# Layer 0's second feed-forward part by seven block products, and its sums of weights copied in batches

## The chip, the cores and the metric

The kernel runs on one core of a Trainium2 chip. The metric is the device time of one execution in microseconds (us); it is taken several times and the median counts. Beside it stands one profiled execution, whose trace gives the start and the duration of each instruction on each engine: PE is TensorE (its matmuls) and PEld its weight loads, DVE is VectorE, ACT ScalarE, POOL GpSimd, and SP the SyncE whose queue issues most DMAs. All products here are fp32 matrices; the reference's tolerance is met by splitting numbers in two, as told below.

## The reference, cut to what matters

Two layers over 512 tokens of width 1024. Layer 0 has a convolution module and then a feed-forward part; layer 1 has windowed attention over a K and V made once, and then a feed-forward part; a norm ends it.

```python
def rmsnorm(x, g):
    xf = x.astype(jnp.float32)
    xf = xf * lax.rsqrt(jnp.mean(xf * xf, axis=-1, keepdims=True) + EPS)
    return (xf * g.astype(jnp.float32)).astype(x.dtype)

def swiglu_ffn(x, w_up, w_down):
    gate, up = jnp.split(x @ w_up, 2, axis=-1)
    return (jax.nn.silu(gate) * up) @ w_down
...
    h = h + swiglu_ffn(rmsnorm(h, norm_ffn[l]), ffn_w_up[l], ffn_w_down[l])
```

`w_up` is 1024 x 5632 (gate and up of 2816 each) and `w_down` 2816 x 1024, one of each for a layer. The change concerns `x @ w_up` of layer 0.

## The kernel before, in words

**Layout and precision.** The residual `h` lies transposed, channels on partitions, 8 tiles of 128 x 512 tokens. Weights lie in DRAM as chunks of 128 x 1024 fp32 (512 KB), in the array `W`. `PLAN` lists the chunks in the order in which PE uses them. For each use `advance` (L274) issues the loads up to nine chunks ahead (`load` L235, on SP, into `raw` buffers, seven of them) and splits chunks up to three ahead (`split_weights` L262): ACT casts `whi` (L263) and DVE subtracts for `wlo` (L266), four buffers of each. `mm3` (L345) then makes one fp32 product of three fp32r matmuls, whi by x-high, whi by x-low, wlo by x-high (L349 to L351). The first chunks (`NATIVE`) are used unsplit, in one fp32 matmul (L347) that reads the raw buffer itself.

**The feed-forward part, a pair at a time.** A pair is 256 of the 2816 hidden columns. Layer 0 takes 11 pairs in two parts (`HALVES0`). Pairs 0 to 4 are done for each half of the tokens as soon as that half's convolution is finished, the first half by `mm3`, the second by `mm2` (L376, two matmuls where one is 512 wide, `twin=True`). Pairs 5 to 10 follow for all 512 tokens at once: `ffn_part(0, 1, x0["ffn0"], ALL, ...)` calls `ffn_up` (L600), which for each pair uses 4 chunks, 8 `mm3` each, 128 x 512 outputs, and then `down_group`.

**Seven products.** Layer 1 (pairs 1 to 10) does the up product by blocks: the weights of a pair are cut in 2 x 2 blocks A11 to A22, the rows of tokens in B11 to B22, and seven products of half the size replace eight (`SEVEN`, L55: A11 B11, S1 T1, S2 T2, A12 B21, S3 T3, S4 B22, A22 T4). T1 to T4 are sums of blocks of x, made once in SBUF by POOL and split by ACT and DVE. S1 to S4 are sums of blocks of weights, made in DRAM by DMA: SP copies one block to a scratch tile (L255) and POOL adds the second by an accumulating DMA (L259). `prepare` (L243) is a generator of those copies and additions; `advance` takes `share[0]` of a step from it for each chunk used. It keeps the addition six steps behind its copy. `seven_pair` (L766) runs the seven products as 168 matmuls of 128 x 256 into three PSUM banks, gathers the four blocks of the result in SBUF (L784 to L796), and applies the norm's scale (L802), silu (L803) and the gate (L804).

**What sets the order.** Instructions are put on the engines' queues by a scheduler that works from the program's order and a modelled time line; each queue then runs in order. `tc.issue_after(x)` keeps an instruction behind another. Side work runs in generators: `job(gen, points)` takes steps from one as chunks are used (`pace` L305), here the convolution of the second half and the reads of the attention bias (`read_bias` L1189). The POOL queue carries arithmetic and the additions' DMAs, so an addition that waits for its copy holds what stands behind it.

**The stages in the trace.** Convolution and its pointwise products up to about 129 us, `pw2` and pairs 0 to 4 of the first half to 265, `pw2` and pairs 0 to 4 of the second half to 362, the up products of pairs 5 to 10 to 493 and their down products to 558, K, V and attention to 718, layer 1's feed-forward part to 1043, the end to 1058. DRAM tables for the bias are written in the convolution stage (`table_in` L1093, `table` L1099: `fd`, 3 MB).

Of the kernel before, what the change touches and what calls it, by code (L numbers as in the profile page):

```python
# [18 lines left out]
P = 128  # L19
# [39 lines left out]
def by_seven(layer, pair):  # L59
    return layer == 1 and pair in SEVENS  # L60
# [56 lines left out]
BLOCKS = [c[:2] + (f"A{a}",) for c in PLAN if len(c) == 3 and c[2] == "S1" for a in (11, 12, 21, 22)]  # L117
# [5 lines left out]
def lay_weights(w):  # L123
    out = np.empty((len(CHUNKS), P, 1024), np.float32)
    q = w["w_q"][0][:, HEAD_COLS]
    o = w["w_o"][0][HEAD_COLS, :]
    for i, c in enumerate(CHUNKS):
        if c[0] == "pw1":
            t = w["conv_w_pw1"][0][:, c[1] * P:(c[1] + 1) * P].reshape(KT, P, P)
        elif is_block(c):  # L130
            m, k = int(c[2][1]) - 1, int(c[2][2]) - 1
            if c[0] == "up":
                t = [w["ffn_w_up"][1][k * 512:(k + 1) * 512, col:col + P].reshape(4, P, P)
                     for col in (e * FF + c[1] * 256 + m * P for e in range(2))]
# [56 lines left out]
def hybrid_trunk(ctx: ExitStack, tc: tile.TileContext, xT, W, prm_in, wdw_in, sinks, relb, onehot, fin, lead, out):  # L191
# [33 lines left out]
    summed, preparing, share, loaded = {}, [iter(())], [0, 0], []  # L225
# [4 lines left out]
    def chunk(c, name=None):  # L230
        if name is not None:
            c = c[:2] + (name,)
        return summed[c] if is_sum(c) else W[CHUNK_AT[c]]

    def load(upto):  # L235
        while stream["dma"] < min(len(PLAN), upto):
            i = stream["dma"]
            r = wpool.tile([P, 1024], F32, tag="raw", name=uid("raw"), bufs=7)
            loaded[:] = [nc.sync.dma_start(r, chunk(PLAN[i])).ins]
            raws[i] = r  # L240
            stream["dma"] += 1

    def prepare():  # L243

        units = [c[:2] for c in PLAN if is_block(c) and c[2] == "S1"]
        adds, todo, before = [], [], None
        for u in units:
            adds += [u + ("S1",), *([before + ("S4",)] if before else []), u + ("S2",), u + ("S3",)]
            before = u
        adds.append(before + ("S4",))  # L250
        for c in adds + [None] * 6:
            if c is not None:
                summed[c] = dpool.tile([P, 1024], F32, tag=uid("sum"), name=uid("sum"))
                with tc.issue_after(loaded[0]):
                    nc.sync.dma_start(summed[c], chunk(c, SUMS[c[2]][0]))  # L255
                todo.append(c)
            if c is None or len(todo) > 6:
                a = todo.pop(0)
                nc.gpsimd.dma_start(summed[a], chunk(a, SUMS[a[2]][1]), accum_op=ALU.add, max_dma_last_dim=4096)  # L259
            yield  # L260
# [132 lines left out]
    both = [wpool.tile([P, 1024], F32, tag="raw", name=uid("both"), bufs=7) for _ in range(KT // 2)]  # L393
# [53 lines left out]
    class Rms:  # L447
# [6 lines left out]
        def add(self, t):  # L454
            sq = temp()[:, 0:self.w]
            self.squared = nc.scalar.square(sq, t).ins
            if self.acc is None:
                self.acc = sq
            else:
                self.eng.tensor_add(sq, self.acc, sq)  # L460
                self.acc = sq

        def step1(self):
# [10 lines left out]
            nc.gpsimd.tensor_tensor(self.rs[:, 0:n], ms[:, 0:n], mhalf[:, 0:n], op=ALU.pow)  # L474
# [77 lines left out]
    def ffn_part(layer, part, xg, tok, rms, on_h=None, twin=False, plain=None):  # L552
# [3 lines left out]
        for g in range(2):  # L556
            if twin:
# [11 lines left out]
                for m, b in enumerate(banks):  # L569
                    t, hm = temp()[:, 0:w], h[g * 4 + m][:, tok]  # L570
                    nc.scalar.copy(t, b[:, 1, :])
                    nc.vector.tensor_add(t, b[:, 0, :], t)
                    nc.gpsimd.tensor_mul(t, t, rs_bc)
                    nc.vector.tensor_add(hm, hm, t)
# [24 lines left out]
    def ffn_up(layer, lo, hi, xg, tok, rms, twin=False, plain=None):  # L599
# [3 lines left out]
        def evac(pair, banks):  # L603
            rs_bc = rms.step2()
            if twin:
# [10 lines left out]
                nc.gpsimd.tensor_mul(t2, t1, t2)  # L616
# [15 lines left out]
            for m in range(2):  # L632
# [4 lines left out]
                nc.gpsimd.tensor_mul(t2, t1, t2)  # L637
# [65 lines left out]
    class Rows:  # L703


        def __init__(self, gain, pool):
# [3 lines left out]
            self.block = {f"B{j + 1}{s + 1}": [q[:, :, HALF[s]] for q in self.x.q[j]] for j in range(2) for s in range(2)}  # L710
# [5 lines left out]
        def sums(self):  # L716
# [7 lines left out]
            for name, t, f, a, b in (("T1", t1, nc.gpsimd.tensor_sub, b11, b12), ("T2", b11, nc.gpsimd.tensor_add, b22, t1),  # L724
                                     ("T3", b12, nc.gpsimd.tensor_sub, b22, b12), ("T4", b21, nc.gpsimd.tensor_sub, b11, b21)):
                f(t, a, b)
                yield
                both = quads.tile([P, 2, 4, 256], F32R, tag="quad", name=uid("rows"))
                self.block[name] = [both[:, a] for a in range(2)]
                split(self.block[name], t, name == "T2")  # L730
# [35 lines left out]
    def seven_pair(pair, rows, pool, between=None):  # L766

        c = new_gates(pool)
        c11, c12, c21, c22 = (c[:, m, s] for m in range(2) for s in range(2))
        chains = {}  # L770
        for n, name in enumerate(SEVEN):
            w = [x.rearrange("p (a k c) -> p a k c", a=2, k=4) for x in get_seven("up", pair, n)]
# [6 lines left out]
            for which in range(2):  # L779
                for k in range(4):  # L780
                    mm3(r[:, which], [v[:, which, k, :] for v in w], [x[e][:, k, :] for e in range(2)],
# [18 lines left out]
        for m in range(2):  # L800
# [3 lines left out]
            nc.gpsimd.tensor_mul(gate, gate, c[:, m, :, 1, :])  # L804
# [4 lines left out]
    def forms_of(c, pool, odd):  # L809
# [7 lines left out]
        for t, a, b in (("T1", "B11", "B12"), ("T3", "B22", "B12"), ("T2", "B22", "T1"), ("T4", "T2", "B21")):  # L817
            (nc.gpsimd.tensor_add if t == "T2" else nc.gpsimd.tensor_sub)(f[:, FORM[t]], f[:, FORM[a]], f[:, FORM[b]])
# [10 lines left out]
    def low_pairs(pair, forms, rs):  # L829

        chains = {}
        for n, name in enumerate(SEVEN):
# [6 lines left out]
            for t, out in enumerate(chains[chain]):  # L839
# [8 lines left out]
                if a == "A12":  # L848
                    m = temp()
                    nc.scalar.mul(m, out, scale)  # L850
                    nc.gpsimd.tensor_add(to, to, m.rearrange("p (i c) -> p i c", i=4))
# [24 lines left out]
    with tc.tile_pool(name="conv", bufs=2) as cv:  # L876
# [41 lines left out]
        class Half:  # L918
# [7 lines left out]
            def taps(self, ct, c):  # L926
# [9 lines left out]
                for i in range(nd):  # L936
                    while pi * nd < n_pool * (i + 1):
# [4 lines left out]
                        else:  # L942
                            on_act = nc.scalar.mul(pr, a[:, j:j + W2], tap(j))  # L943
                            on_pool = nc.gpsimd.tensor_add(pr, acc, pr)  # L944
# [10 lines left out]
                nc.gpsimd.tensor_add(yt, yt, acc)  # L955
# [137 lines left out]
        def table_in():  # L1093
            nc.sync.dma_start(sk, sinks.to_broadcast([P, NH]))
            nc.sync.dma_start(lhs[0:NBUCKET, :], relb)
            nc.sync.dma_start(oh, onehot)
            nc.gpsimd.memset(lhs[NBUCKET:NBUCKET + 1, :], NEG)

        def table():  # L1099
# [4 lines left out]
            nc.sync.dma_start(fd.rearrange("q h k -> h q k"), fs.unsqueeze(1).to_broadcast([NH, P, 3 * P]))  # L1104
# [77 lines left out]
        pw2(h0.z, n0)  # L1182
        ffn_part(0, 0, x0["ffn0"], HALF[0], n0.rms, plain=plain)
        flush()

    attn = ExitStack()
    at = attn.enter_context(tc.tile_pool(name="attn", bufs=2))
# [11 lines left out]
    base = seen[0]  # L1199
# [6 lines left out]
    class Both:  # L1206
        def step1(self):
            pass
# [3 lines left out]

    nxt = Next(("kv", "mix1"))


    share[0] = 1 / 2
    if True:
        ffn_part(0, 1, x0["ffn0"], ALL, Both(), nxt.on_h)
# [60 lines left out]
        def pair(gp, jp, n0):  # L1279
# [33 lines left out]
            for (n, k0, nk), sc, m4 in zip(units, scs, m4s):  # L1313
# [6 lines left out]
                for j in range(4):  # L1320
                    nc.gpsimd.tensor_scalar(sc[:, j, 1:1 + w], sc[:, j, 1:1 + w], sm[:, j:j + 1], 0.0,
                                            op0=ALU.mult, op1=ALU.add)
# [104 lines left out]
    share[0] = 1 / 3  # L1427
    for kind, pair in STEPS1:
# [6 lines left out]
        if by_seven(1, pair):  # L1435
            c = seven_pair(pair, nxt, pool7, flip if pair == SEVENS[0] else None)
# [70 lines left out]
```

## Time and profile before

| | |
|---|---|
| runs | 1059.93, 1061.91, 1062.57 us; median 1061.91 |
| the profiled execution | 1060.15 us, span 1058.4 us from the first to the last instruction |
| granted TensorE clock | 0.996 |
| matmuls in the trace | 6166 |
| DMA | 211.04 MB in packets, mean 199 GB/s |

The profile page gives busy times, the span in 40 slices, the DMA queues, the chain of waits that ended last, and the costliest groups of instructions. A group's line reads: source line, engine, operation, output and inputs, shape, count; then busy time and the mean of one in ns; then the idle time before them and what ended it. A plain fp32 matmul stands in the trace as two records, an fp32r one as one.

### The profile page before, as it was taken

How to read it: one execution, taken by the hardware profiler on the slowest of the kernel's cores; microseconds unless marked ns; L12 is line 12 of the kernel's file. 1: busy time of each engine (PE TensorE's matmuls, PEld its weight loads, DVE VectorE, ACT ScalarE, POOL GpSimd, SP SyncE). 2: the span in 40 equal slices, each digit the busy share in tenths (PEclk: the TensorE clock that was granted, in tenths of full speed). 3: DMA queues.
4: the chain of work that ended last, by engine and by line, in shares of the span. 5: the costliest groups of instructions: out<-in, count | busy, mean ns of one | idle time of the engine just before them, and what ended most of it. 6: DMA issues, size and time to landing. Idle time of an engine off the chain costs nothing.

```text
span 1058.4 us, 16667 instructions
## 1 busy us (share of the span) xinstructions
PE 1046.2 (99%) x6166; PEld 923.3 (87%) x6166; DVE 737.6 (70%) x1163; ACT 576.6 (54%) x1008; POOL 437.8 (41%) x535
## 2 busy tenths in 40 slices
PE   9999999999999999999999999999999999999996
PEld 8888889999988888888888877778989999898995
DVE  3999988977866654454427466678678777868677
ACT  3887897854645423322325465556655555554653
POOL 3999999810333312221124255305242323323131
PEclk9999999999999999999999999999999999999998
DMA  9438045577999996767779876765799565555532
GB/s 354 153 96 98 7 140 199 182 225 218 278 291 293 327 256 183 213 164 192 204 210 247 239 199 172 187 164 170 239 274 305 185 196 174 170 194 183 195 121 80
DMA packets 56606, 211.04 MB, mean 199 GB/s; under 512 B 6891, under 2 KB 13196, under 8 KB 55564
## 3 DMA queue, kind: packets, MB, share of 16 engines
q1 hardware_dynamic: 47164, 177.42, 49.8%
q0 software_dynamic: 8640, 31.46, 16.9%
q8 instruction: 48, 0.79, 0.3%
q10 hardware_dynamic: 720, 1.10, 0.3%
q14 instruction: 34, 0.28, 0.1%
HBM read 204.71 MB, written 68.16 MB: 258 GB/s over the span
## 4 chain that ended last, share of the span: by engine, by line
PE 89%; ACT 4%; issue 2%; POOL 2%; DVE 1%; DMA 1%; SPq 0%; ACTq 0%; POOLq 0%
PE bank L349 19%; PE bank L351 19%; PE bank L350 19%; PE bank L844 9%; PE bank L902 8%; PE bank L381 5%; PE bank L382 3%; ACT pr L943 1%; PE bank L1302 1%; PE bank L1344 1%; PE bank L1331 1%; PE bank L1000 1%; DMA sum<-in_W_dram 1%; POOL pr L944 1%; DMA both<-in_lead_dram 1%
## 5 line engine op out<-in xcount | busy, mean ns | idle before, releaser
L266 DVE TENSOR_TENSOR wlo<-raw,whi 128x1024 fp32r<-128x1024 f32 x231 | 305.8, 1332 | 166.1 <-ACT whi L263 165.1
L263 ACT CAST whi<-raw 128x1024 fp32r<-128x1024 f32 x231 | 241.2, 1049 | 274.8 <-PE bank L350 194.4
L349 PE MATMUL bank<-quad,whi 128*128 128x256 f32 (+1 forms) x976 | 326.9, 336 | 0.0
L350 PE MATMUL bank<-quad,whi 128*128 128x256 f32 (+1 forms) x976 | 326.0, 334 | 0.0
L351 PE MATMUL bank<-quad,wlo 128*128 128x256 f32 (+1 forms) x976 | 326.0, 334 | 0.0
L349 PEld LDWEIGHTS bank<-quad,whi 128*128 128x128 f32 x976 | 185.3, 190 | 19.8 <-issue 1.6
L351 PEld LDWEIGHTS bank<-quad,wlo 128*128 128x128 f32 x976 | 185.3, 190 | 18.8 <-issue 0.6
L350 PEld LDWEIGHTS bank<-quad,whi 128*128 128x128 f32 x976 | 185.4, 190 | 18.4 <-issue 0.2
L944 POOL TENSOR_TENSOR pr<-pr,pr 128x256 f32<-128x256 f32 x208 | 159.0, 798 | 3.8 <-ACT pr L943 3.8
L951 DVE SCALAR_TENSOR_TENSOR bank<-apad,wdw,bank 128x256 f32<-128x256 f32 x248 | 112.3, 484 | 3.3
L943 ACT ACTIVATE pr<-apad,wdw 128x256 f32<-128x256 f32 x208 | 98.2, 501 | 15.4 <-POOL pr L944 13.2
L804 POOL TENSOR_TENSOR up<-up 128x512 f32<-128x512 f32 x20 | 35.4, 1769 | 162.2 <-ACT up L803 162.2
L902 PE MATMUL bank<-quad,w 128*128 128x256 f32 x448 | 98.7, 380 | 0.0
L259 POOL DMA_DIRECT2D sum<-in_W_dram x30 | 25.0, 832 | 174.1 <-DMA sum<-in_W_dram 152.4
L902 PEld LDWEIGHTS bank<-quad,w 128*128 128x128 f32 x448 | 84.9, 190 | 11.8 <-DVE bank L951 0.2
L349 PE MATMUL bank<-rows,whi 128*128 128x256 f32 x320 | 90.8, 284 | 0.5 <-ACT up L788 0.5
L351 PE MATMUL bank<-rows,wlo 128*128 128x256 f32 x320 | 90.6, 283 | 0.0
L350 PE MATMUL bank<-rows,whi 128*128 128x256 f32 x320 | 90.5, 283 | 0.0
L259 POOL DMA_DIRECT2D sum<-sum x30 | 24.7, 823 | 140.7 <-DMA sum<-in_W_dram 128.4
L381 PE MATMUL bank<-quad,whi 128*128 128x512 f32 x212 | 76.0, 398 | 0.0
L349 PEld LDWEIGHTS bank<-rows,whi 128*128 128x128 f32 x320 | 61.4, 192 | 0.9 <-ACT up L788 0.7
L350 PEld LDWEIGHTS bank<-rows,whi 128*128 128x128 f32 x320 | 61.4, 192 | 0.3
(218 smaller groups left out, 1642.9 us busy)
## 6 DMA issues: line engine op xcount, KB each, us to landing
raw<-in_W_dram SPq DMA_DIRECT2D x183, 512.0 KB, 4.2
sum<-in_W_dram SPq DMA_DIRECT2D x60, 512.0 KB, 5.8
raw<-sum SPq DMA_DIRECT2D x60, 512.0 KB, 4.4
sum<-in_W_dram POOLq DMA_DIRECT2D x30, 512.0 KB, 7.0
sum<-sum POOLq DMA_DIRECT2D x30, 512.0 KB, 7.5
w<-in_W_dram SPq DMA_DIRECT2D x14, 512.0 KB, 9.3
fd<-fs SPq DMA_DIRECT2D x1, 3072.0 KB
h<-in_xT_dram SPq DMA_DIRECT2D x8, 256.0 KB, 8.4
```

Of the source, the lines that this page charges most:

```text
L259: nc.gpsimd.dma_start(summed[a], chunk(a, SUMS[a[2]][1]), accum_op=ALU.add, max_dma_last_dim=4096)
L263: on_act = nc.scalar.copy(hi, src).ins
L266: latest[:] = [on_act, lo_engine[0].tensor_sub(lo, src, f32(hi)).ins]
L349: nc.tensor.matmul(out, w[0], x[0], start=start, stop=False, **kw)
L350: nc.tensor.matmul(out, w[0], x[1], start=False, stop=False, **kw)
L351: nc.tensor.matmul(out, w[1], x[0], start=False, stop=stop, **kw)
L381: nc.tensor.matmul(first[2], first[0], first[1], start=start, stop=False)
L844: nc.tensor.matmul(out, x, w[:, ws], start=first and e == 0 and i == 0, stop=e == 1 and i == 2, skip_group_check=True)
L902: mm = nc.tensor.matmul(self.pb[:, w * W2:(w + 1) * W2], w1_of(ct, w, k), x[k] if x else xg[k][:, tok], start=k == 0, stop=k == KT - 1)
L943: on_act = nc.scalar.mul(pr, a[:, j:j + W2], tap(j))
L944: on_pool = nc.gpsimd.tensor_add(pr, acc, pr)
L951: on_dve = nc.vector.scalar_tensor_tensor(yt if i == nd - 1 else c, src, tap(i), c if i else self.shift, op0=ALU.mult, op1=ALU.add)
```

## The change

Pairs 5 to 10 of layer 0 go to `seven_pair`, with kind `up0`; a class `Rows0` gives them their blocks of x and makes T1 to T4 by a job during the second half's pairs 0 to 4, from plain fp32 copies of the scaled x (`plain` for the first half, which was there, and `plain1`, which is new and is filled by one more ACT operation in `Next.on_h`). T1 to T3 and the results of a pair lie in a pool `part2` of five 8 KB buffers, T1's plain form in a `raw` buffer; the pool of the attention opens after it, and the bias reads move behind it. There are now 21 units of weights (6 of layer 0, 15 of layer 1), 84 sums in place of 60. The copies of the first six units are four DMAs of 3 MB in `table_in`, those of units 6 to 8 four DMAs of 1.5 MB in `table`; the rest are single, six additions ahead. The additions start with the first half's pairs 0 to 4, and each is kept behind the last POOL instruction written before it. The raw buffers are six.

```diff
 def by_seven(layer, pair):
-    return layer == 1 and pair in SEVENS
+    return pair in SEVENS if layer else pair >= HALVES0[1][0]
...
-            plan.extend(ups(layer, pair))
+            plan.extend(blocks_of("up0", pair) if by_seven(layer, pair) else ups(layer, pair))
...
+UNITS = [c[:2] for c in PLAN if is_block(c) and c[2] == "S1"]
+EARLY = (0, sum(u[0] == "up0" for u in UNITS), 9)
...
-            r = wpool.tile([P, 1024], F32, tag="raw", name=uid("raw"), bufs=7)
+            r = wpool.tile([P, 1024], F32, tag="raw", name=uid("raw"), bufs=6)
...
+    def pool_op(op):
+        pooled[0] = op.ins
+        return op
+
+    def copy_sums(name, lo, hi):
+
+        i = CHUNK_AT[UNITS[lo] + (SUMS[name][0],)]
+        t = dpool.tile([P, hi - lo, 1024], F32, tag=uid("sum"), name=uid("sum"))
+        for k in range(lo, hi):
+            summed[UNITS[k] + (name,)] = t[:, k - lo]
+        return nc.sync.dma_start(t, W[i:i + hi - lo].rearrange("u p c -> p u c")).ins
+
     def prepare():
-        for c in adds + [None] * 6:
-            if c is not None:
-                summed[c] = dpool.tile([P, 1024], F32, tag=uid("sum"), name=uid("sum"))
-                with tc.issue_after(loaded[0]):
-                    nc.sync.dma_start(summed[c], chunk(c, SUMS[c[2]][0]))
-                todo.append(c)
-            if c is None or len(todo) > 6:
-                a = todo.pop(0)
-                nc.gpsimd.dma_start(summed[a], chunk(a, SUMS[a[2]][1]), accum_op=ALU.add, max_dma_last_dim=4096)
+        todo = []
+        for r in range(len(UNITS) + 2):
+            todo += [UNITS[u] + (s,) for s, u in (("S1", r), ("S3", r - 1), ("S2", r - 1), ("S4", r - 2))
+                     if 0 <= u < len(UNITS)]
+        for n, c in enumerate(todo):
+            for ahead in todo[n + 6:n + 7]:
+                if ahead not in summed:
+                    with tc.issue_after(loaded[0]):
+                        copy_sums(ahead[2], UNITS.index(ahead[:2]), UNITS.index(ahead[:2]) + 1)
+            with tc.issue_after(pooled[0]):
+                nc.gpsimd.dma_start(summed[c], chunk(c, SUMS[c[2]][1]), accum_op=ALU.add, max_dma_last_dim=4096)
+            added.add(c)
             yield
...
-    def seven_pair(pair, rows, pool, between=None):
+    def seven_pair(kind, pair, rows, c, between=None):
...
+            if kind == "up0":
+                nc.vector.tensor_mul(c[:, m, :, 1, :], c[:, m, :, 1, :], rs_bc)
+            pool_op(nc.gpsimd.tensor_mul(gate, gate, c[:, m, :, 1, :]))
...
         def table_in():
-            nc.sync.dma_start(oh, onehot)
+            behind = nc.sync.dma_start(oh, onehot).ins
+            for name in SUMS:
+                with tc.issue_after(behind):
+                    behind = copy_sums(name, *EARLY[0:2])
...
         def table():
-            nc.sync.dma_start(fd.rearrange("q h k -> h q k"), fs.unsqueeze(1).to_broadcast([NH, P, 3 * P]))
+            behind = nc.sync.dma_start(fd.rearrange("q h k -> h q k"), fs.unsqueeze(1).to_broadcast([NH, P, 3 * P])).ins
+            for name in SUMS:
+                with tc.issue_after(behind):
+                    behind = copy_sums(name, *EARLY[1:3])
...
+        preparing[0], share[0] = prepare(), 0.4
         ffn_part(0, 0, x0["ffn0"], HALF[0], n0.rms, plain=plain)
...
+    class Rows0:
+        def sums(self):
+            b11, b12, b21, b22 = (f[:, j * 4:j * 4 + 4] for j in range(2) for f in self.f)
+            t1 = wpool.tile([P, 4, 256], F32, tag="raw", name=uid("t1"), bufs=6)
+            for n, (name, t, f, a, b) in enumerate((
+                    ("T1", t1, nc.gpsimd.tensor_sub, b11, b12), ("T2", b11, nc.gpsimd.tensor_add, b22, t1),
+                    ("T3", b12, nc.gpsimd.tensor_sub, b22, b12), ("T4", b21, nc.gpsimd.tensor_sub, b11, b21))):
+                pool_op(f(t, a, b))
+                yield
+                if n < 3:
+                    both = z0.tile([P, 2, 4, 256], F32R, tag="z0", name=uid("rows"), bufs=5)
+                else:
+                    both = quads.tile([P, 2, 4, 256], F32R, tag="quad", name=uid("rows"))
+                self.block[name] = [[both[:, e, k] for k in range(4)] for e in range(2)]
+                split([both[:, e] for e in range(2)], t, name == "T2")
+                yield
...
-    job(chain(*(read_bias(*b) for b in ((0, 0), (0, 1), (1, 0)))), (base, 0), (base + 30, 7))
-    preparing[0], share[0] = prepare(), 1 / 3
-    n1 = Next(("ffn0",), x0, bc0, HALF[1])
+    plain1 = z0.tile([P, KT, W2], F32, tag="z0", name=uid("plain1"), bufs=5)
+    n1 = Next(("ffn0",), x0, bc0, HALF[1], plain=plain1)
+    job(rows0.sums(), (base + 16, 0), (base + 36, 9))
     pw2(h1.z, n1)
     ffn_part(0, 0, x0["ffn0"], HALF[1], n1.rms, twin=True)
...
-    share[0] = 1 / 2
-        ffn_part(0, 1, x0["ffn0"], ALL, Both(), nxt.on_h)
+    share[0] = 1 / 4
+    for pair in range(lo0, hi0):
+        c = seven_pair("up0", pair, rows0, z0.tile([P, 2, 2, 2, 256], F32, tag="z0", name=uid("up"), bufs=5))
+        for m in range(2):
+            split([d.rearrange("p (s q) -> p s q", s=2) for d in hid0[2 * (pair - lo0) + m]], c[:, m, :, 0, :])
+    part2.close()
+
+    attn = ExitStack()
+    at = attn.enter_context(tc.tile_pool(name="attn", bufs=2))
+    job(chain(*(read_bias(*b) for b in ((0, 0), (0, 1), (1, 0)))), (seen[0], 0), (seen[0] + 10, 7))
+    share[0] = 0.6
+        for g in range(2):
+            banks = accs(512)
+            down_group([(("down", 0, kp, g), 2 * (kp - lo0)) for kp in range(lo0, hi0)], lambda kt: hid0[kt], banks)
...
-    share[0] = 1 / 3
+    share[0] = 1 / 4
```

More of the change, by code (lines that the diff above doesn't have):

```diff
@@ L224, in hybrid_trunk @@
     latest = []
-    summed, preparing, share, loaded = {}, [iter(())], [0, 0], []
+    summed, added, preparing, share, loaded, pooled = {}, set(), [iter(())], [0, 0], [], [None]
     def is_sum(c):
@@ L232, in chunk @@
             c = c[:2] + (name,)
-        return summed[c] if is_sum(c) else W[CHUNK_AT[c]]
+        if not is_sum(c):
+            return W[CHUNK_AT[c]]
+        assert c in added
+        return summed[c]
     def load(upto):
@@ L391, in hybrid_trunk @@
     w1 = [None] + [quads.tile([P, 2, KT, P], F32, tag="quad", name=uid("w1")) for _ in range(1, KT)]
-    both = [wpool.tile([P, 1024], F32, tag="raw", name=uid("both"), bufs=7) for _ in range(KT // 2)]
+    both = [wpool.tile([P, 1024], F32, tag="raw", name=uid("both"), bufs=6) for _ in range(KT // 2)]
     x_first = [both[k // 2][:, k % 2 * 512:k % 2 * 512 + 256] for k in range(KT)]
@@ L709, in __init__ @@
             self.x = Act(KT)
-            self.block = {f"B{j + 1}{s + 1}": [q[:, :, HALF[s]] for q in self.x.q[j]] for j in range(2) for s in range(2)}
+            self.block = {f"B{j + 1}{s + 1}": [[q[:, k, HALF[s]] for k in range(4)] for q in self.x.q[j]]
+                          for j in range(2) for s in range(2)}
         def on_h(self, i):
@@ L771, in seven_pair @@
         for n, name in enumerate(SEVEN):
-            w = [x.rearrange("p (a k c) -> p a k c", a=2, k=4) for x in get_seven("up", pair, n)]
+            w = [x.rearrange("p (a k c) -> p a k c", a=2, k=4) for x in get_seven(kind, pair, n)]
             a, b = name.split()
@@ L780, in seven_pair @@
                 for k in range(4):
-                    mm3(r[:, which], [v[:, which, k, :] for v in w], [x[e][:, k, :] for e in range(2)],
+                    mm3(r[:, which], [v[:, which, k, :] for v in w], [x[e][k] for e in range(2)],
                         first and which == 0 and k == 0, which == 1 and k == 3, skip_group_check=True)
@@ L1199, in hybrid_trunk @@
+    part2 = ExitStack()
+    z0 = part2.enter_context(tc.tile_pool(name="part2", bufs=5))
+    plain1 = z0.tile([P, KT, W2], F32, tag="z0", name=uid("plain1"), bufs=5)
+    n1 = Next(("ffn0",), x0, bc0, HALF[1], plain=plain1)
     base = seen[0]
[L1200 to L1202 removed]
+    rows0 = Rows0(x0["ffn0"], plain, plain1)
+    rows0.rms = rows0
```

66 lines of the change are left out of this document (33 added, 33 removed).

## The prediction, as put on record before the result

> **What bounds the kernel now.** I read the page first (busy times, then the slices), then what the weight loads waited for, then the chain of waits stretch by stretch.
>
> ```profile
> span 1058.4 us, 16667 instructions
> PE 1046.2 (99%) x6166; PEld 923.3 (87%) x6166; DVE 737.6 (70%) x1163; ACT 576.6 (54%) x1008; POOL 437.8 (41%) x535
> PE   9999999999999999999999999999999999999996
> PEclk9999999999999999999999999999999999999998
> DMA  9438045577999996767779876765799565555532
> PE 89%; ACT 4%; issue 2%; POOL 2%; DVE 1%; DMA 1%; SPq 0%; ACTq 0%; POOLq 0%
> ```
>
> PE is busy in every slice at the full granted clock, and no other engine comes near it; DMA has one hole early and is full later.
>
> ```profile
> PEld L1296 <- issue: 2.8, 8, 0.4
> ...
> PEld bank L349 <- ACT up L788: 0.7, 1, 0.7
> ```
>
> The dearest wait of the weight loads is 2.8 us in all, so no stall is worth removing. Time can only be won by fewer or shorter matmuls, and lost where a matmul begins to wait. The profiled execution took 1060.15 us, 1.75 more than its span; the median of the runs is 1061.91, 1.76 above it. I make the sum against the profiled one and add 1.76 at the end.
>
> **What is removed and added on PE.** The up products of pairs 5 to 10 of layer 0 are 6 pairs x 4 chunks x 8 `mm3` x 3 = 576 matmuls 512 wide, between these two pieces of the chain (start, duration):
>
> ```profile
> 362.38 0.23 PE bank L349
> ...
> 492.94 0.23 PE bank L349
> ```
>
> That is 130.56 us, or 0.2267 for each. In their place come 6 pairs x 7 products x 8 `mm3` x 3 = 1008 matmuls 256 wide. Layer 1 shows their price, in a period of two seven-product pairs (336 matmuls) and one `low` group (84 matmuls 512 wide, 72 of which are the two pieces at L844):
>
> ```profile
> 836.63 5.52 PE bank L844 x24
> ...
> 845.02 11.09 PE bank L844 x48
> ...
> 896.34 5.52 PE bank L844 x24
> ```
>
> The period is 896.34 - 836.63 = 59.71. One 512-wide matmul costs (5.52 + 11.09)/72 = 0.2307, 84 of them 19.38; the remaining 40.33 over 336 gives 0.1200. So 1008 x 0.1200 = 121.0 us come for 130.6 that go: **-9.6 us** (a pair takes 168 x 0.1200 = 20.2).
>
> That needs the other engines to keep up in the new stage:
>
> ```profile
> 363.50:494.00 130.50, 130.50 (x578) 108.05 (x577) 59.90 (x63) 39.31 (x48) 28.92 (x29) 1.00 0.77 214
> 910.90:970.60 59.70, 59.70 (x422) 56.11 (x421) 44.74 (x49) 32.59 (x42) 17.30 (x15) 1.00 0.58 185
> L266 DVE TENSOR_TENSOR wlo<-raw,whi 128x1024 fp32r<-128x1024 f32 x231 | 305.8, 1332 | 166.1 <-ACT whi L263 165.1
> L263 ACT CAST whi<-raw 128x1024 fp32r<-128x1024 f32 x231 | 241.2, 1049 | 274.8 <-PE bank L350 194.4
> L802 DVE TENSOR_TENSOR up<-up,rsbc 128x512 f32<-128x512 f32 x20 | 13.6, 680 | 0.0
> L803 ACT ACTIVATE up<-up 128x512 f32<-128x512 f32 x20 | 12.7, 633 | 11.4 <-DVE up L802 11.4
> ```
>
> The first two are stretches by engine (length, then PE, PEld, DVE, ACT and POOL busy, clock, DMA share, GB/s): the stage that goes, and one period of layer 1. There PE lacks nothing in 59.70 us while DVE works 44.74. A new pair has per 20.2 us on DVE 7 splits of weights (7 x 1.332), three gathers, two scalings of the gate, two new scalings of the other half and two splits of the result, nine operations of about 0.68: some 15.4 us. On ACT 7 x 1.049 and eight operations of under 0.65 make about 12.3. Both fit, DVE at 76%, about as in the period shown (75%). Weights per pair are seven loads plus four copies and additions; the old stage ran at a DMA share of 0.77 and had four loads a pair with its additions, the period shown 0.58. I take the stage as bound by PE.
>
> In one sentence beside this, which the sum does without: the Trainium skill ("TensorE: Matmul & The Clock Gate", The mechanism, in Part 3) says that a weight load overlaps matmuls in flight only when its row group differs, by which 432 more loads of full height would add to the time. The trace does not agree: in the second stretch loads are busy 56.11 and matmuls 59.70 of the same 59.70 us.
>
> **One wait that I expect to be new.** Before pair 0 of the second half is scaled, the norm's sums go PE (L470), DVE, POOL, ACT (L482), PE (L496):
>
> ```profile
> 285.30 0.50 PE L470 MATMUL bank<-ones_c,tmp 128*128 128x1 f32 x4
> 286.08 0.72 POOL L474 TENSOR_TENSOR rs<-ms,mhalf 128x2 f32<-128x2 f32 x1 [0.43 <-DVE ms L472]
> 287.29 0.69 ACT L482 ACTIVATE tmp<-ident,rs 128x128 f32<-128x128 f32 x2
> 288.32 0.59 PE L496 MATMUL bank<-tmp,ones_m 128*128 128x256 f32 x2
> ```
>
> From the end of the column sums (285.80) to the spread it took 2.52 us, with ACT late (it began 0.49 after `rs` ended at 286.80); the least it can take is about 287.49 - 285.80 = 1.7. The order of instructions of the changed kernel puts three matmuls in this place where there were sixteen, because ACT has eight more scalings for `plain1` and the sums come later. Three cover 3 x 0.2267 = 0.68. So PE waits 1.0 to 1.8 us; ACT being fuller, I take **+1.6**, and 0 to 2.5 as ends.
>
> **Edits that I cost at nothing, and their cover.**
>
> The batched copies. Four DMAs of 3.146 MB stand on SP's queue behind `oh`, four of 1.573 MB behind `fd`; all raw loads for `pw2` beyond the first six stand behind them (six buffers now, not seven).
>
> ```profile
> q1 hardware_dynamic: 47164, 177.42, 49.8%
> q0 software_dynamic: 8640, 31.46, 16.9%
> sum<-in_W_dram SPq DMA_DIRECT2D x60, 512.0 KB, 5.8
> 30.27 0.34 SPq L1096 DMA_DIRECT2D oh<-in_onehot_dram  x1
> 73.91 0.34 SPq L1104 DMA_DIRECT2D fd<-fs  x1
> 36.00:68.00 32.00, 32.00 (x151) 28.22 (x151) 31.14 (x79) 26.06 (x56) 32.00 (x47) 1.00 0.04 17
> 73.00:106.00 33.00, 33.00 (x155) 29.05 (x154) 31.16 (x73) 26.67 (x61) 33.00 (x49) 1.00 0.90 126
> 131.57 3.62 PE L347 MATMUL bank<-z,raw 128*128 128x256 f32 x16
> 133.49 3.78 SPq L239 DMA_DIRECT2D raw<-in_W_dram  x2
> ```
>
> The hole (36 to 68) is where the first four run, `fd` fills about 30 us after 73.91, then come the others. Chunk 6 of `pw2` can be loaded when chunk 0 frees its buffer (133.5), and PE, at 3.62 us a chunk, wants it five chunks later, at 151; with 3 us for the load, the copies must be through by 148. They move 18.87 MB. At the rate of q1 in its busy time, 177.42/(0.498 x 1058.4) = 337 GB/s, the first four end at 31.5 + 37 = 69, the others at 104 + 19 = 123: nothing lost. At the rate of q0, 31.46/(0.169 x 1058.4) = 176 GB/s, all end at 61.5 + 107 = 168.7, and PE waits for 20.7 us. (One single copy alone, 512 KB in 5.8 us, gives 90 GB/s, but that holds the latency of a DMA, which a batch pays once.) I take the first: these are plain copies on q1. The 512 KB of a copy are 128 rows of 4 KB, as a raw load's are.
>
> POOL in the second half's convolution and after. Additions now stand among POOL's operations, each kept behind the one written before it:
>
> ```profile
> L259 POOL DMA_DIRECT2D sum<-sum x30 | 24.7, 823 | 140.7 <-DMA sum<-in_W_dram 128.4
> sum<-sum POOLq DMA_DIRECT2D x30, 512.0 KB, 7.5
> 217.18 2.41 POOL L955 TENSOR_TENSOR y<-y,pr 128x256 f32<-128x256 f32 x2 [7.70 <-DVE y L951]
> 226.50 0.71 POOL L1022 TENSOR_TENSOR rr<-var,mhalf 128x2 f32<-128x2 f32 x1 [3.85 <-DVE var L1016]
> 227.87 0.69 ACT L1027 ACTIVATE tmp<-ident,rr 128x128 f32<-128x128 f32 x2
> 231.16 0.86 PE bank L1031 x2
> ```
>
> Six among the taps cost 6 x 0.82 = 5 us, and POOL idles 7.70 before the last additions to `y`. Seven then stand before `rr`; the last adds onto an accumulation that is issued at about 219.6 and lands 7.5 later (227.1), then its own 0.83, `rr` 0.71 and ACT 0.69 give 229.3, against 231.16 when PE takes it. 1.9 us spare.
>
> T1 to T4 on POOL among the second half's pairs 0 to 4. The same sums in layer 1:
>
> ```profile
> L726 POOL TENSOR_TENSOR quad<-quad,quad x2: 3386/3388/3390, 722.4 to 725.7; 128x1024 f32<-128x1024 f32 x2
> L726 POOL TENSOR_TENSOR t<-quad x1: 2410/2410/2410, 717.5 to 717.5; 128x1024 f32<-128x1024 f32 x1
> ```
>
> 11.6 us in all, put in singly over twenty chunks; a pair's result there comes up to 8 us late for them, and PE has three chunks of work ahead, about 8.5 us. This cover is the thinnest. The bias reads, moved to the down products, need no PE. The sums of weights are led by twenty chunks or more.
>
> **Sum.** -9.6 + 1.6 = -8.0: 1060.15 - 8.0 = 1052.15 for the profiled execution, **1053.9** beside the median.
>
> **The rivals.**
>
> *The batches hold up the raw loads* (slower). One mechanism: SP's queue is in order, chunk 6 of `pw2` comes late. It costs nothing above 18.87 MB/(148 - 61.5) = 218 GB/s, eats the gain at 200 (8 us late, through at 156) and gives 1053.9 + 20.7 = 1074.6 at 176. For it: the rows of a unit lie 512 KB from the next, and these are DRAM-to-DRAM as q0's are. Against: q0's additions read a third stream. 10%.
>
> The Trainium skill ("DMA: Bandwidth & Descriptors", row "HBM row pitch at large powers of two") gives 207 GB/s for copies with a pitch of 512 KiB; by it the copies would end at 152.7, PE would wait 4.7, and an estimate by that page is 1058.6. No row of this profile shows such a copy.
>
> *POOL's order holds a result back.* An addition before `rr`, or a T sum before a gate, waits longer than its cover: 3 to 7 us, 1056.9 to 1060.9. For it: the covers of 1.9 and about 0.5 us above. Against: waits of PE on POOL are nearly absent now, though POOL waits 128.4 us for copies. 13%.
>
> *Seven products are no faster here*, the splits falling behind at seven in 20.2 us so that the -9.6 goes: 1063. Against: the period of layer 1 with the same density. 3%.
>
> **Chances and range.** The forecast holds at 74%, the rivals at 10, 13 and 3. A measurement of this kernel tells 0.3%, 3.2 us, from no change: under 1058.7 is faster, over 1065.1 slower. Faster: 0.74 + half of POOL's rival 0.07 = 0.81. Slower: nearly all of the batches' rival and a little of the third, 0.11. The rest 0.08. The forecast alone goes from 1050.5 (no new wait at the norm, and small waits of layer 1 going) to 1055. The range takes POOL's rival in and leaves out the batches' and the third, 13%: 1050.0 to 1061.0.
>
> **What would show it.** The up stage of pairs 5 to 10 lasting 121 us without gaps; a gap of about 1.6 us on PE ahead of the norm's spread near 288; no wait of PE for a raw buffer near 151; none at `pw2` near 231 and none for `up` among the second half's pairs 0 to 4. A raw load landing after 151, or a gate behind a T sum on POOL with PE idle, would show the rivals. The number would also be wrong if the `low` group's other 12 matmuls cost more than 0.2307, since 0.1200 hangs on it.

## The result, and the profile after

| | before | changed |
|---|---|---|
| median of five runs | 1061.91 us (1059.82 to 1065.62) | 1056.86 us (1055.94 to 1058.22) |
| ratio to before | | 0.9947 (95%: 0.9924 to 0.9970) |
| profiled execution, span | 1060.15, 1058.4 | 1057.85, 1056.0 |

The kernel became faster by 5.0 us where 8.0 were forecast. The two profiled executions lie only 2.3 us apart: that of before is a quick one among its runs, that of after a late one. So the parts below, which are read from the two traces, make up 2 us and not 5.

The page of the changed kernel, busy times and slices:

```profile
span 1056.0 us, 17739 instructions
PE 1039.9 (98%) x6598; PEld 938.2 (89%) x6598; DVE 781.6 (74%) x1203; ACT 614.1 (58%) x1062; POOL 476.4 (45%) x563
PE   9999999999998999999999999999999999999996
```

The 13th slice (317 to 343 us) is the only 8 in PE's row. What the weight loads waited for there is the view to read next (total, times, longest):

```profile
PEld bank L396 <- DVE wlo L280: 3.9, 3, 2.9
PEld bank L512 <- ACT tmp L498: 3.1, 2, 2.7
PEld L1362 <- issue: 2.8, 8, 0.4
```

In the kernel before, the rows of the same two places were:

```profile
PEld bank L496 <- ACT tmp L482: 0.5, 1, 0.5
PEld bank L382 <- DVE wlo L266: 0.4, 1, 0.4
```

Both waits have grown from half a us or less. L396 is the second half's pairs 0 to 4 (the two-matmul product), waiting for the low part of a weight split; L512 is the spread of the norm. By stretches, the second half's pairs 0 to 4 before and after, and the seven-product stage (length, then PE, PEld, DVE, ACT, POOL busy, clock, DMA share, GB/s):

```profile
276.60:362.20 85.60, 85.60 (x488) 74.24 (x487) 59.80 (x73) 47.22 (x78) 31.40 (x29) 1.00 0.96 295
```

```profile
276.50:371.10 94.60, 89.37 (x488) 76.69 (x487) 77.88 (x79) 53.43 (x85) 45.13 (x35) 0.96 0.89 241
...
371.26:488.70 117.44, 117.44 (x986) 117.44 (x985) 83.67 (x97) 65.01 (x86) 29.16 (x24) 1.00 0.86 256
```

The same 488 matmuls take 9.0 us longer. The seven-product stage has no gap: 984 of its 1008 matmuls lie in it (the last product is put behind the first down product), 0.1193 each, so 120.3 us for all, against 130.56 before: -10.3. The rest of the kernel gave -0.7. -10.3 + 9.0 - 0.7 = -2.0, by which the last matmul is earlier.

**The wait at 288.** The chain from the norm's column sums to its spread, in the changed kernel:

```profile
287.66 0.16 DVE L488 TENSOR_SCALAR ms<-bank 128x2 f32<-128x2 f32 x1 [1.84 <-PE bank L486]
...
287.90 0.71 POOL L490 TENSOR_TENSOR rs<-ms,mhalf 128x2 f32<-128x2 f32 x1 [2.74 <-DVE ms L488]
...
288.04 1.99 ACT L277 CAST whi<-raw 128x1024 fp32r<-128x1024 f32 x2 [4.41 <-issue]
289.94 0.69 ACT L498 ACTIVATE tmp<-ident,rs 128x128 f32<-128x128 f32 x2
...
290.69 0.79 PE L512 MATMUL bank<-tmp,ones_m 128*128 128x256 f32 x1 [2.27 <-ACT tmp L498]
```

`rs` is ready at 288.6, but two weight casts stand ahead of the diagonal on ACT until 290.0. And PE does not come back at full speed:

```profile
290.70:294.40 3.70, 3.70 (x12) 3.12 (x13) 2.10 (x5) 2.01 (x6) 1.28 (x1) 0.56 0.92 302
...
327.40:331.30 3.90, 3.89 (x15) 3.36 (x15) 3.90 (x3) 1.94 (x3) 1.10 (x1) 0.59 1.06 259
```

The eighth number is the granted clock: 0.56 and 0.59 in the four us after the two long waits, 1.00 elsewhere in this stage. So a wait of 2.4 us costs 4.0 here. (From here on a loss is what the distances between the starts of matmuls sum to beyond their usual ones, 0.12 to 0.24 us by shape.) The two waits at 318 and 324 cost 5.2 in the same way (0.8 and 4.4).

**The waits at 318 and 324.** DVE and POOL at that place:

```profile
308.27 10.61 DVE L280 TENSOR_TENSOR wlo<-raw,whi 128x1024 fp32r<-128x1024 f32 x2
318.81 1.22 DVE L528 TENSOR_TENSOR rows<-t,rows 128x1024 fp32r<-128x1024 f32 x1
...
324.30 5.28 DVE L280 TENSOR_TENSOR wlo<-raw,whi 128x1024 fp32r<-128x1024 f32 x2
```

```profile
311.62 2.98 POOL L1241 TENSOR_TENSOR plain<-plain,t 128x1024 f32<-128x1024 f32 x1
313.95 1.41 POOL L272 DMA_DIRECT2D sum<-in_W_dram  x1
314.52 3.27 POOL L1241 TENSOR_TENSOR plain<-plain 128x1024 f32<-128x1024 f32 x1
```

```profile
327.41 0.39 PE L396 MATMUL bank<-quad,wlo 128*128 128x256 f32 x1 [2.45 <-DVE wlo L280]
```

And all splits of 305 to 331 us in the view of their line (minimum, median, maximum in ns):

```profile
L280 DVE TENSOR_TENSOR wlo<-raw,whi x7: 1209/2306/7287, 305.5 to 330.6; 128x1024 fp32r<-128x1024 f32 x7
```

A split takes 1.2 us alone. Two of them take 10.6 while POOL makes T1 to T3 (L1241; one of the two 7.29, through T2 and T3), and two more 5.3, beside T4 and a product of POOL's behind it. DVE counts as busy all that time: the page's share says nothing of it, the duration of one instruction does. In the view of waits PE is held by DVE, not by a gate that is late on POOL, which was the rival that I had priced.

### The profile page after: what moved, and what is told of

It reads as the page before. It is cut to its first block, busy times and chain, and to the rows that moved or that the text cites. A ratio compares the mean times of both kernels' runs of the same rounds, so it can differ in the third digit from the quotient of the medians.

```text
span 1056.0 us, 17739 instructions
## 1 busy us (share of the span) xinstructions
PE 1039.9 (98%) x6598; PEld 938.2 (89%) x6598; DVE 781.6 (74%) x1203; ACT 614.1 (58%) x1062; POOL 476.4 (45%) x563
## 4 chain that ended last, share of the span: by engine, by line
PE 87%; DVE 4%; ACT 3%; issue 3%; POOL 2%; DMA 0%; POOLq 0%; DVEq 0%; ACTq 0%
PE bank L363 19%; PE bank L365 19%; PE bank L364 19%; PE bank L862 9%; PE bank L920 7%; PE bank L395 4%; PE bank L396 2%; DVE wlo L280 1%; PE bank L1368 1%; ACT pr L961 1%; PE bank L1410 1%; PE bank L1397 1%; POOL pr L962 1%; DVE bank L969 1%; PE bank L908 1%
## 5 line engine op out<-in xcount | busy, mean ns | idle before, releaser
L280 DVE TENSOR_TENSOR wlo<-raw,whi 128x1024 fp32r<-128x1024 f32 x249 | 337.7, 1365 | 136.4 <-ACT whi L277 134.6
L277 ACT CAST whi<-raw 128x1024 fp32r<-128x1024 f32 x249 | 260.0, 1048 | 277.0 <-PE bank L364 179.5
L363 PE MATMUL bank<-quad,whi 128*128 128x256 f32 (+1 forms) x928 | 292.3, 317 | 0.0
L365 PE MATMUL bank<-quad,wlo 128*128 128x256 f32 (+1 forms) x928 | 291.7, 315 | 0.0
L364 PE MATMUL bank<-quad,whi 128*128 128x256 f32 (+1 forms) x928 | 291.6, 315 | 0.0
L822 POOL TENSOR_TENSOR up<-up 128x512 f32<-128x512 f32 x32 | 56.5, 1764 | 281.2 <-ACT up L819 281.2
L363 PE MATMUL bank<-rows,whi 128*128 128x256 f32 x512 | 144.7, 283 | 0.0
L364 PE MATMUL bank<-rows,whi 128*128 128x256 f32 x512 | 144.6, 283 | 0.0
L365 PE MATMUL bank<-rows,wlo 128*128 128x256 f32 x512 | 144.5, 283 | 0.0
L364 PEld LDWEIGHTS bank<-rows,whi 128*128 128x128 f32 x512 | 97.8, 191 | 0.3
L363 PEld LDWEIGHTS bank<-rows,whi 128*128 128x128 f32 x512 | 97.7, 191 | 0.3
L365 PEld LDWEIGHTS bank<-rows,wlo 128*128 128x128 f32 x512 | 97.6, 191 | 0.0
L474 POOL TENSOR_TENSOR tmp<-tmp,tmp 128x256 f32<-128x256 f32 (+1 forms) x28 | 27.4, 979 | 105.0 <-ACT tmp L470 102.9
```

What stands on the lines that cost most here:

```text
L277: on_act = nc.scalar.copy(hi, src).ins
L280: latest[:] = [on_act, lo_engine[0].tensor_sub(lo, src, f32(hi)).ins]
L363: nc.tensor.matmul(out, w[0], x[0], start=start, stop=False, **kw)
L364: nc.tensor.matmul(out, w[0], x[1], start=False, stop=False, **kw)
L365: nc.tensor.matmul(out, w[1], x[0], start=False, stop=stop, **kw)
L822: pool_op(nc.gpsimd.tensor_mul(gate, gate, c[:, m, :, 1, :]))
```

## The experiments

All with their own runs of the kernel before beside them (medians 1061.4 to 1063.0); ratios are to those.

**T1 to T4 on DVE.**

```diff
-  ("T1", t1, nc.gpsimd.tensor_sub, b11, b12), ("T2", b11, nc.gpsimd.tensor_add, b22, t1), ...
-  pool_op(f(t, a, b))
+  ("T1", t1, nc.vector.tensor_sub, b11, b12), ("T2", b11, nc.vector.tensor_add, b22, t1), ...
+  f(t, a, b)
```

> T1 to T4 are made by DVE in place of POOL, all else as in the changed kernel. Lock theory: POOL's sums stood in the way of DVE's weight splits (one split took 7.29 us from 311.59, another 3.05 from 324.30, beside 1.2 elsewhere); with them gone the waits of PE at 318 and 324 and the slow clock after them go, 0.77 + 4.38 us of the changed kernel's profile, while the wait of 2.4 us at 288 stays: about 1052, 3 to 5 us under the changed kernel, and splits of 1.2 us between 305 and 330. Rival, DVE is simply overloaded there: DVE gets 4 x 1.2 us more of its own work and the waits stay or grow: 1056 to 1059.

1052.95 us, ratio 0.9906 (0.9888 to 0.9924). The waits for `wlo` are gone, the wait of 2.4 us for the norm stays. DVE, which got the work, has room for it; it was held, not full.

**plain1 filled behind the norm.**

```diff
-    n1 = Next(("ffn0",), x0, bc0, HALF[1], plain=plain1)
+    n1 = Next(("ffn0",), x0, bc0, HALF[1])
+    def fill():
+        for i in range(KT):
+            with tc.issue_after(n1.rms.last_mul), tc.issue_after(latest[0]):
+                nc.scalar.mul(plain1[:, i, :], h[i][:, HALF[1]], col("ffn0", i))
+            yield
...
+    job(fill(), (base + 13, 0), (base + 16, 9))
```

> The eight scalings that fill plain1 are put behind the second half's norm on ACT, T1 to T4 stay on POOL. Theory of the prediction (these scalings make the column sums late): sixteen matmuls again between the column sums and the spread, the wait at 288 (2.4 us, 4.0 with the slow clock after it) goes, the waits at 318 and 324 stay: about 1053, 3 to 4 under the changed kernel. Rival, the additions in POOL's written order make the norm late: the wait at 288 stays above 1.5 us and the time within 1 us of the changed kernel's.

1053.62 us, ratio 0.9914 (0.9895 to 0.9932). The wait at 288 is gone, those for `wlo` stay (4.2 us in the view of waits). The additions in POOL's order stayed as they were, so by themselves they do not make this wait.

**Both.**

> Both edits together: T1 to T4 on DVE and plain1 behind the norm. If the two losses are separate and are all that kept the gain from being the 10 us of the products: both go, the second half's pairs 0 to 4 take as long as before the change (85.6 us from first to last of their matmuls), about 1049 to 1050. If the losses only move elsewhere: 1052 to 1056.

1048.42 us (1048.14 to 1048.79), ratio 0.9865 (0.9847 to 0.9882): the fastest version of the study, 8.4 under the changed kernel. That is 1.3 more than the 3.9 and 3.2 of the two edits alone; what the 1.3 are, the runs do not separate. In its trace the pairs 0 to 4 of the second half are back at their old length, although DVE and ACT do more there:

```profile
276.50:362.10 85.60, 85.60 (x492) 74.65 (x491) 70.32 (x82) 55.94 (x92) 34.58 (x32) 1.00 0.95 264
```

**Is it POOL's queue, or what POOL reads?** Two ways to put POOL's work back without its result. First by memsets:

```diff
     f(t, a, b)
+    for _ in range(6):
+        pool_op(nc.gpsimd.memset(scratch, 0.0))
```

> T1 to T4 on DVE, and at each of their places POOL writes a scratch tile by six memsets of 128x512, so that POOL's queue is held for about as long as by its sums (2.4 to 3.4 us each) without reading SBUF. Lock theory: DVE's splits aren't held, the time is that of T1 to T4 on DVE within 1 us. Rival, what counted is POOL's queue (gates that stand behind the sums): the waits at 318 to 331 come back, 3 to 5 us over T1 to T4 on DVE.

1054.37 us, ratio 0.9920 (0.9902 to 0.9938), but it tells nothing of the question: with no operand to wait for, the memsets ran from 230.1 to 257.8, long before T1. Three of them stood ahead of the convolution's `rr`, and PE waited for that:

```profile
230.10 1.99 POOL L1244 MEMSET scratch<- 128x512 f32 x3
232.06 0.71 POOL L1040 TENSOR_TENSOR rr<-var,mhalf 128x2 f32<-128x2 f32 x1
```

```profile
233.54 0.96 PE L1049 MATMUL bank<-tmp,ones_m 128*128 128x512 f32 x1 [1.96 <-ACT tmp L1045]
```

So the cover ahead of `rr` is thin: 2 us of POOL too much there, and PE lost 3.8 in this execution (2.1, and again a stretch at clock 0.57). It was the slowest of its five (1056.87); the median lies only 1.4 over T1 to T4 on DVE. The second try, on the kernel with both edits, ties the scratch work to its place and asks the question twice:

```diff
     f(t, a, b)
+    nc.vector.tensor_copy(scratch[:, 0:1], t[:, 3, 255:256])
+    for _ in range(6):
+        pool_op(nc.gpsimd.memset(scratch, 0.0))
```

> From the kernel with both edits (1048.42): after each of T1 to T4 (made by DVE) POOL writes a scratch tile by six memsets of 128x512, tied to the place by one column that DVE writes first; about 3.1 us of POOL each (0.525 a memset in the run before), no SBUF read. Lock theory: DVE's splits stay near 1.2 us beside the memsets, no wait of PE at 314 to 325, 1048 to 1050. Rival, POOL's occupied queue is what cost PE 5.3 us: the waits come back, 1052 to 1054.

and in the other kernel

```diff
     f(t, a, b)
+    nc.vector.tensor_copy(scratch[:, 0:1], t[:, 3, 255:256])
+    for u in (slice(0, 2), slice(2, 4)):
+        pool_op(nc.gpsimd.tensor_sub(scratch.rearrange("p (k c) -> p k c", k=2), a[:, u], b[:, u]))
```

> The same, but POOL's scratch work reads SBUF: two subtractions of 128x512 of the same blocks after each of T1 to T4, whose result nobody uses. Lock theory: DVE's two-input operations that meet it take 2 to 7 us in place of 1.2 and PE waits again for wlo, 2 to 5 us over the memsets: 1050 to 1054. Rival (queue): the same as the memsets, within 1 us.

Memsets: 1048.67 us, ratio 0.9863 (0.9841 to 0.9884), the time of the kernel without them. Subtractions that read SBUF: 1051.86, ratio 0.9892 (0.9872 to 0.9911), 3.4 us more, and PE waits for `wlo` again. DVE beside the memsets, then beside the subtractions:

```profile
306.79 3.46 POOL L1245 MEMSET scratch<- 128x512 f32 x6 [4.20 <-DMA raw<-in_W_dram]
...
306.65 1.21 DVE L1242 TENSOR_TENSOR plain<-plain,t 128x1024 f32<-128x1024 f32 x1
307.78 1.22 DVE L1242 TENSOR_TENSOR plain<-plain 128x1024 f32<-128x1024 f32 x1
```

```profile
307.07 4.44 POOL L1245 TENSOR_TENSOR scratch<-plain,plain 128x512 f32<-128x512 f32 x2 [4.22 <-DVE scratch L1243]
...
308.04 2.31 DVE L280 TENSOR_TENSOR wlo<-raw,whi 128x1024 fp32r<-128x1024 f32 x1
310.28 0.74 DVE L628 TENSOR_TENSOR tmp<-bank,tmp 128x256 f32<-128x256 f32 x2
```

A DVE instruction with two inputs in SBUF goes at 1.21 beside POOL's writing, and takes 2.31 when it meets POOL's reading; the additions of L628, with one input in PSUM, go on at 0.4 each beside it. (The subtractions differ from the memsets in two more ways: they are 4.4 us at a place and not 3.5, and once DVE waits for one to end before it may overwrite a block, 0.5 us.) The Trainium skill says just this ("SBUF — State Buffer", Who interferes with whom): a DVE instruction with two SBUF inputs contends with a GpSimd instruction that reads SBUF, not with one that only writes it. The runs agree, and it is the rule that the prediction should have weighed.

**Does it help to cut POOL's sums in pieces?** On the kernel with `plain1` later:

```diff
-    pool_op(f(t, a, b))
+    for k in range(4):
+        pool_op(f(t[:, k], a[:, k], b[:, k]))
```

> From the kernel with plain1 later (1053.62, T1 to T4 on POOL): each sum in four instructions of 128x256 in place of one of 128x1024. If the lock is held for an instruction, DVE gets in between: splits of at most 2 to 2.5 us, most of the 5.3 us of waits at 314 to 325 goes: 1049 to 1051. If POOL and DVE only share a bandwidth, or POOL's next instruction keeps the lock: no change, 1053 to 1055.

1053.67 us, ratio 0.9908 (0.9889 to 0.9927): no change. One DVE instruction stands through a whole row of POOL's pieces:

```profile
310.21 7.17 DVE L528 TENSOR_TENSOR rows<-t,rows 128x1024 fp32r<-128x1024 f32 x1 [1.71 <-ACT rows L527]
```

```profile
310.84 1.32 POOL L1242 TENSOR_TENSOR plain<-plain 128x256 f32<-128x256 f32 x1
311.54 1.31 POOL L1242 TENSOR_TENSOR plain<-plain,t 128x256 f32<-128x256 f32 x1
...
315.56 2.38 POOL L1242 TENSOR_TENSOR plain<-plain 128x256 f32<-128x256 f32 x1
316.82 2.94 POOL L1242 TENSOR_TENSOR plain<-plain 128x256 f32<-128x256 f32 x1
```

The same section of the Trainium skill says, of DVE instructions in its two-port modes, that whoever issues first holds the pair of ports for the whole instruction; a split or a sum of two tensors has no such mode by that section. Here DVE did not get in between POOL's instructions, eight pieces and two DMA issues long, while beside the scratch subtractions above it got in after one (2.31 us). What decides that, the traces don't show.

**The second part of the change alone** (batches, order and six raw buffers; layer 0's pairs 5 to 10 by eight products, no T's and no `plain1`):

```diff
-    return pair in SEVENS if layer else pair >= HALVES0[1][0]
+    return layer == 1 and pair in SEVENS
...
-EARLY = (0, sum(u[0] == "up0" for u in UNITS), 9)
+EARLY = (0, 6, 9)
...
-    class Rows0: ...
+        ffn_part(0, 1, x0["ffn0"], ALL, Both(), nxt.on_h)
```

> The second part of the change alone: copies in batches (four of 3 MB and four of 1.5 MB, now all of layer 1's units), single additions later and in POOL's written order, six raw buffers; layer 0's pairs 5 to 10 by eight products as before the change, without plain1 and T1 to T4. If the seven products alone bring the gain (10 to 11 us on PE): 1059 to 1061, at or just under the kernel before. If batching and order bring a part: under 1058. If they cost something that the products hide: over 1063.

1062.29 us, ratio 0.9998 (0.9983 to 1.0013): as a whole and by itself this part changes nothing that the runs can tell. The time lies just over the 1059 to 1061 that I gave for this case. The next two take it away from the kernel with both edits.

**No batches**, all 84 sums copied singly:

```diff
-            behind = nc.sync.dma_start(oh, onehot).ins
-            for name in SUMS:
-                with tc.issue_after(behind):
-                    behind = copy_sums(name, *EARLY[0:2])
+            nc.sync.dma_start(oh, onehot)
...
-            for ahead in todo[n + 6:n + 7]:
+            for ahead in todo[n + 6 if n else 0:n + 7]:
```

> From the kernel with both edits (1048.42): no batches, each of the 84 sums is copied singly, six additions ahead, as before the change. If the batches matter to PE (they take copies out of a stretch whose DMA share is near 1): raw loads come late in the second half's pairs 0 to 4 or in the stage of the seven products, waits of PE for whi or wlo, 1051 to 1056. If the loads' nine chunks of lead absorb it: 1048 to 1050, and the batches bought nothing here.

1059.43 us, ratio 0.9981 (0.9969 to 0.9993), 11 us over the kernel with them, more than I had given the case for it; and not where I looked: the waits lie at 179 to 228, in the first half's stage, where the single copies now share SP's queue with the raw loads.

```profile
190.00:210.00 20.00, 16.00 (x125) 14.98 (x124) 14.79 (x22) 15.96 (x27) 14.28 (x15) 1.00 1.04 344
210.00:230.00 20.00, 16.98 (x127) 15.74 (x126) 19.56 (x24) 10.27 (x17) 10.03 (x13) 1.00 1.00 340
```

DMA is full there, a raw load lands 11.0 us after its issue in the median (185 to 260 us; 6.7 with the batches), and splits come late. Whether the order of SP's queue does it or the bandwidth that the copies take, this run does not separate.

**Additions not kept in POOL's written order:**

```diff
-            with tc.issue_after(pooled[0]):
+            with nullcontext():
                 nc.gpsimd.dma_start(summed[c], ...)
```

> From the kernel with both edits: the additions are not kept behind the last POOL instruction written before them, so the scheduler puts them where it sees room. If the written order protects POOL's arithmetic (the norm and the gates) from additions that wait for copies: waits of PE at the norms or gates, 1050 to 1055. If it is neutral: 1048 to 1050.

1150.35 us, ratio 1.0833 (1.0810 to 1.0856): far beyond the case that I gave. The scheduler puts additions ahead of the convolution's arithmetic, where they wait for their copies:

```profile
158.11 2.53 POOL L272 DMA_DIRECT2D sum<-in_W_dram  x3 [18.82 <-DMA sum<-in_W_dram]
```

and the view of waits counts (total, times, longest)

```profile
POOL sum L272 <- DMA sum<-in_W_dram: 286.8, 47, 19.1
...
PE bank L1018 <- POOL y L973: 43.0, 2, 41.3
PE bank L989 <- POOL y L973: 27.0, 3, 15.6
```

| kernel | us | ratio |
|---|---|---|
| changed | 1056.86 | 0.9947 |
| T1 to T4 on DVE | 1052.95 | 0.9906 |
| plain1 behind the norm | 1053.62 | 0.9914 |
| both | 1048.42 | 0.9865 |
| both, POOL memsets tied to T1 to T4 | 1048.67 | 0.9863 |
| both, POOL reads tied to T1 to T4 | 1051.86 | 0.9892 |
| plain1 behind the norm, sums in quarters | 1053.67 | 0.9908 |
| batches and order, eight products | 1062.29 | 0.9998 |
| both, single copies | 1059.43 | 0.9981 |
| both, additions unordered | 1150.35 | 1.0833 |

## Why the prediction was right, and where its sizes were wrong

The direction and the range (1050.0 to 1061.0) held; the forecast was 3.0 us too fast. That it was no more is in part luck. Between the two profiled executions the gain is 2.3 us where the sum said 8.0, since two waits cost some 7.6 us more than forecast, while the products and the rest gave 1.4 more. The other 2.7 us come from the spread of the runs: I added 1.76 to get from the profiled execution to the median, and the changed kernel's median lies 0.99 under its profiled one.

- **The products, -9.6**: measured -10.3, at 0.1193 a matmul in place of 0.1200, with no gap in the stage. Right.
- **The new wait at the norm, +1.6**: its place and its cause were right (shown by the fill behind the norm), its size was not: 4.0. The wait itself was 2.4, because two casts of 1.0 stood before the diagonal on ACT and not one, and the slow clock after it added 1.6; my price of a wait was its length alone.
- **T1 to T4 on POOL, 0** ("PE has three chunks of work ahead"): this is the step that failed, 5.2 us. I asked what stands behind the sums on POOL and found that the gates had cover. I did not ask what POOL's reading does to DVE, and used the splits (two SBUF inputs) at their mean of 1.332. The trace of before had the sign. By its starts and ends, 159 of the 231 splits meet no arithmetic of POOL's, and none of these took over 1.23 us; of the 72 that meet it, 35 took over 1.4, up to 2.69. One of them, and POOL beside it:

```profile
302.82 2.31 DVE L266 TENSOR_TENSOR wlo<-raw,whi 128x1024 fp32r<-128x1024 f32 x1
302.76 1.29 POOL L614 TENSOR_TENSOR tmp<-tmp,rsbc 128x512 f32<-128x512 f32 x1 [2.12 <-DVE tmp L612]
```

- **Batches, 0**: right. They ran at 327 GB/s, and PE never waited for a raw load behind them:

```profile
107.00:126.00 19.00, 19.00 (x92) 16.46 (x91) 18.15 (x48) 14.12 (x35) 19.00 (x29) 1.00 0.99 327
```

  I had them through at 123; DMA was full up to 126. The Trainium skill's 207 GB/s ("DMA: Bandwidth & Descriptors", row "HBM row pitch at large powers of two") was not seen here, and the run is no test of it: that row is for a pitch of 512 KiB from partition to partition, while here the rows of the partitions lie 4 KB apart in `W` and only the units 512 KB. What I missed is that without the batches the same products would hardly have paid (1059.43, with both edits).
- **POOL ahead of `rr`, 0**: right in its effect, but the cover was thinner than the 1.9 us of the sum. The diagonal was ready at 230.6, not 229.3, and PE took it 0.3 later:

```profile
229.89 0.70 ACT L1045 ACTIVATE tmp<-ident,rr 128x128 f32<-128x128 f32 x2 [2.00 <-POOL rr L1040]
230.92 1.02 PE L1049 MATMUL bank<-tmp,ones_m 128*128 128x512 f32 x2
```

- **The rivals**: POOL's order holding a gate back (13%) had the measured time at the edge of its range (1056.9 to 1060.9), by another mechanism than the one that ran: what was held was DVE.

## What to carry to other kernels

An engine's work moved to POOL is not free because POOL is idle: look at what DVE does beside it, and give POOL only work that doesn't read SBUF while DVE has instructions with two SBUF inputs on the path. Price a wait of PE of about two us or more with a slow stretch of clock that may follow it. And a scheme that adds transfers is to be judged with the stage in which they run: batches, order and six raw buffers together were worth nothing without the seven products, and the batches 11 us beside them.

## What the hardware showed that I had not expected

- DVE's two-input instruction can wait not for one POOL instruction but for a row of them: 7.17 us through the quarters, 7.29 through T2 and T3.
- Waits of 2.4 to 2.6 us at 288 and 324 were each followed by about 4 us at a clock of 0.56 to 0.60, and so was one of 2.1 at 231; one of 2.1 at 317 (the quarters) and one of 2.0 at 213 (single copies) were not, the clock stayed at 1.00. The Trainium skill ("TensorE: Matmul & The Clock Gate", Why this matters for your kernels) warns of gaps over about 3 us; here shorter ones were enough. In these traces the place of the wait decides, and not its length alone: the clock changes only in steps of 3.41 us (in the changed kernel it is 0.50 from 290.53 to 293.94 and from 328.08 to 331.49, eleven steps apart). The wait at 288 lies almost wholly in one step, that of the quarters across two. The changed kernel:

```profile
287.12:290.53 3.41, 1.29 (x8) 0.82 (x6) 1.57 (x3) 2.49 (x4) 0.71 (x1) 1.00 1.04 255
290.53:293.94 3.41, 3.25 (x9) 2.79 (x10) 2.27 (x5) 1.78 (x7) 1.28 (x1) 0.50 0.91 290
```

  The quarters:

```profile
315.18:318.60 3.42, 2.13 (x13) 1.57 (x11) 3.42 (x4) 2.62 (x3) 3.42 (x6) 1.00 1.02 176
318.60:322.01 3.41, 2.78 (x16) 2.37 (x16) 3.41 (x4) 2.32 (x4) 3.41 (x5) 1.00 1.02 172
```

  The changed kernel's PE idled 2.12 us (3.41 - 1.29) within a step and got half the clock in the next; in the quarters it idled 1.29 and 0.63 and kept the full one. Between the first 10 us and the last matmul, every slow stretch followed a step with 1.9 us of idle or more, and no step with 1.4 or less was followed by one. (The kernel with additions unordered has the two cases between: 1.73 was followed by one, 1.76 was not.) The steps begin at another point in each trace. So the same wait may cost 2.4 us in one execution and 4.0 in another; that is inferred, since each kernel has one trace.
